# A two-direction RWKV-7 scan whose stage becomes one list of single operations

## The chip, the cores and the metric

The kernel runs on one core of a Trainium2 chip. The metric is the device time of one execution in microseconds (us), lower is better. The core's engines work side by side and each runs its own instructions in order: TensorE (PE in the profile, PEld for its weight loads), VectorE (DVE), ScalarE (ACT), GpSimd (POOL), and SyncE (SP), which here only issues DMAs. They wait for one another through semaphores. Matmul results land in PSUM, which has eight banks; the kernel hands them out through three pools: `pm` with two banks, `p2` with two, `pS` with four.

## The reference

One layer of a hybrid model on 128 context tokens and 2048 latent tokens, model width 1024:

- An RMS norm with modulation, then one input projection to eight parts of 512 channels: r, k, v, a gate, and four parts of a short gated convolution.
- Head group A (8 heads of 64 channels) is RWKV-7 time mixing, run once forwards and once backwards over the tokens. For each head a 64x64 state S is carried along: `S = S*w - (S kk)(kk*a)^T + v k^T`, and the output is `y = S r`. The two directions are summed and normalised per head; a bonus term and the gate follow.
- Both groups are joined, pass an output projection, a gated residual and a last RMS norm.

Outputs are y for all tokens and the final context states. Everything is float32.

## The kernel before, in words

Phase 1 makes the projections and writes the scan's operands to DRAM. Phase 2 is the scan. Phase 3 is the output projection; it begins inside the last three stages of the scan.

The scan runs in chunks of 64 tokens. There are 17 stages; one stage does 8 chunks for two heads in each direction, so it has two groups, 0 (forwards) and 1 (backwards). Stages go through 4 head pairs x 4 token blocks, with the context stage put in as the 16th. Inside a chunk the recurrence is turned into matrix products. For each stage:

- **M** (`partM`): per group three products from the loaded operand tile `rr` (1 MB for a group): G, F (16 matmuls each in the program) and the transpose Q; VectorE masks G and F out of PSUM, ScalarE copies Q and half of F. A small tile `dg` collects diagonal blocks of G.
- **I** (`partI`): inverts triangular 32x32 blocks. VectorE transposes `dg` into `ab` (L852); everything else is on GpSimd: the first values of `zt` (L857, L858, L860, L861), two products over 512 columns that turn `ab` (L863, L864), and 15 steps of one product (L868) and two subtractions (L871).
- **Z, c, U** (`partZ`, `partc`, `partU`): VectorE turns the inverse back into `zr`, `zd` (L916, L919); U and W are two rounds of 32 small matmuls each (L934, L941) with ScalarE copies after each, which merge blocks of 32 into 64.
- **B** (`partB`): X (L953) applies the inverse, with 8 negating ScalarE copies (L717); then eight operator tiles E of eight matmuls each (L967), each masked out of PSUM by VectorE (L968).
- **S** (`partS`): the recurrence proper. For each of 8 steps and each group, 4 matmuls E x state into `psS` (L1006), and one VectorE multiply that scales the new state into `sv` (L1019). After four steps the outputs of a group are in one bank and go to the tile `y`, by a ScalarE copy the first time a place is written, and by a VectorE addition (L1036) the second time.
- **f** (`finish`): when the four pieces of a block's `y` are there, the block is finished: square (ACT), sum per head (DVE L1070), root (ACT), reciprocal and multiply (DVE L1074, L1075), transpose on PE into `psT` (L1087), then two VectorE operations (L1090, L1092) and a store. Since the directions meet in the middle, no block is complete in the first two stages of a head pair, two are in the third and two in the fourth.

The trace counts each matmul of the program twice (an E tile is x16 there, an S step of both groups x16).

The order is written by hand: within `manual_schedule` PE, DVE and ACT run exactly in program order (the stages 0 to 13; set-up and the last three stages are placed by the framework's scheduler). The main loop goes through one stage at a time. After each of the 8 recurrence steps it takes a few pieces of the other parts, as the strings of `ORDER` say: `b` and `B` are pieces of this stage's and the next one's B, `M`, `I` belong to the stage three ahead, `Z` to the one two ahead, `W`, `U` to the next, `a` starts a waiting finish and `f` advances it by one piece. A piece is a product with its evictions, or a pair of E tiles. U, W, half of X, and all E tiles use the two banks of `p2`; M uses `pm`; S and T use `pS`.

Of the kernel before, what the change touches and what calls it, by code (L numbers as in the profile page):

```python
# [6 lines left out]
F32 = mybir.dt.float32  # L7
# [612 lines left out]
NST = 17  # L620
MORD = (("GD", 0), ("Q", 0), ("GD", 1), ("Q", 1), ("F", 0), ("F", 1))
ON_DVE = ""
LA = 3


ORDER = ("cbWUMf", "fabMWbM", "IMUflw", "fMBfyr", "Bf", "fam", "fZ", "fByNf")
LAST = ("cbUf", "bbWwf", "fWUf", "fy", "Bff", "Bfm", "ffZf", "Byf")


def phase2(K):  # L630
# [150 lines left out]
    def partL(s, gis=(0, 1)):  # L781
        if s not in sts:
            sts[s] = Ctx()
            sts[s].g = []
        st = sts[s]
        for gi in gis:
            d, units, blk = stages[s][gi]
            g = Ctx()
            st.g.append(g)
            g.d, g.units, g.blk = d, units, blk  # L790
            g.rr = B.rr()
            if blk is None:
                for k in range(4):
                    load(g.rr[:, k], d, k, units, FULL)
            else:
                p, c0 = units[0]
                src = S[f"ops{d}"][:, p * 128:(p + 1) * 128, c0 * 64:(c0 + 8) * 64]
                D(g.rr[:, 0:4].rearrange("p k u t -> p k (u t)"), src.rearrange("k p t -> p k t"))

    def partM(s, st):  # L800

        st.dg = tl([128, 16, 32], "dg", 1, O.rI)
        for gi, g in enumerate(st.g):
            g.F, g.GA, q = B.slots[s % LA][gi]
            g.Q = q[:]

        def pieces(gi, g):

            d, rr = g.d, g.rr

            def tiles(dst, w, x):

                for a in range(4):
                    for h, hr_ in enumerate((H0, H1)):
                        for e, er in enumerate((H0, H1)):
                            u = 2 * a + e
                            T.matmul(dst(h, a, er), w[hr_, u, :], x(hr_, u), start=True, stop=True)  # L817

            def banks(nm):
                return [O.pm.tile([128, 4, 128], F32, tag="m", name=f"ps{nm}{s}_{gi}_{h}") for h in range(2)]  # L820

            def transposes():
                ps = banks("Q")
                tiles(lambda h, a, er: ps[h][er, a, 0:64], rr[:, 3], lambda hr_, u: rr[hr_, 4, u, :])
                for h in range(2):
                    copy("q", g.Q[:, h * 4:h * 4 + 4], ps[h][:, :, 0:64])

            def product(dst, w, x, mask, nm, c0):
                ps = banks(nm)
                tiles(lambda h, a, er: ps[h][er, a, :].rearrange("p (a b) -> p a b", b=64), w, lambda hr_, u: x[hr_, :, u, :])  # L830
                for h in range(2):
                    if c0:
                        copy("f", dst[:, h * 4:h * 4 + 4, 0:c0], ps[h][:, :, 0:c0])
                    V.tensor_tensor(dst[:, h * 4:h * 4 + 4, c0:], ps[h][:, :, c0:], mask[:, c0:].unsqueeze(1).broadcast_to((128, 4, 128 - c0)), ALU.mult)  # L834

            def blocks():
                V.scalar_tensor_tensor(st.dg[:, gi * 8:gi * 8 + 8], g.GA[:, :, 96:128], B.hm[:, 1:2], g.GA[:, :, 64:96], ALU.mult, ALU.add)

            F = lambda: product(g.F, rr[:, 0], rr[:, 4:1:-2], B.msk[:, MF[d]], "F", 64)
            GA = lambda: product(g.GA, rr[:, 3], rr[:, 1::-1], B.mkg[:, MG[d]], "G", 0)  # L840
            return dict(Q=transposes, F=F, G=GA, D=blocks)

        ops = [pieces(gi, g) for gi, g in enumerate(st.g)]
        for piece, gi in MORD:
            for c in piece:
                ops[gi][c]()
            yield

    def partI(s, st):

        ab = tl([128, 32, 32], "ab", 2, O.rI)
        V.transpose(ab[:].rearrange("p j i -> p i j"), st.dg[:].rearrange("p u i -> p i u").unsqueeze(2).broadcast_to((128, 32, 2, 16)))  # L852
        zt = st.zt = tl([128, 16, 32], "zt", 2, O.rI)
        zf = zt[:].rearrange("p a b -> p (a b)")
        tmp = tl([128, 512], "ztmp", 1, O.rI)
        dg = tl([128, 16], "dgp", 1, O.rI)
        G.memset(zt[:], 0.0)  # L857
        G.tensor_copy(zf[:, 0:512:34], B.ph[:, 0:1].broadcast_to((128, 16)))  # L858

        G.tensor_copy(dg[:], ab[:].rearrange("p j i -> p (j i)")[:, 1:1024:66])  # L860
        G.tensor_scalar(zf[:, 1:512:34], dg[:], B.ph[:, 2:3], B.ph[:, 1:2], ALU.mult, ALU.add)  # L861
        tv = tmp[:].rearrange("p (j m) -> p j m", m=16)
        G.tensor_tensor(tv, ab[:, :, 0:32:2], dg[:].unsqueeze(1).broadcast_to((128, 32, 16)), ALU.mult)  # L863
        G.tensor_tensor(ab[:, :, 1:32:2], ab[:, :, 1:32:2], tv, ALU.subtract)  # L864
# [21 lines left out]
    def partw(s, st):  # L886

        for g in st.g:
# [5 lines left out]
            if g.blk is None or c != (2 if d == 0 else 33):  # L894
                continue
# [493 lines left out]
```

## Time and profile before

| what | us |
|---|---|
| median of three timed runs (1738.21 to 1746.28) | 1741.99 |
| the profiled execution's own time | 1734.39 |
| its span, first to last instruction | 1732.3 |
| scan, first to last state multiplication of all 17 stages (starts) | 1043.7 to 1591.3 |
| first S step of stage 0 to first S step of stage 14 (the 14 stages ordered by hand) | 407.0 |

Of the span PE is busy 91%, DVE 64%, ACT 45% and POOL 34%, but the phases differ, so these are read by stretches. The views used are: busy time by stretches (one row for each stretch: its length, then each engine's busy time and instruction count, the granted TensorE clock, the DMA share and GB/s), groups of instructions by line (busy time, mean ns of one, and the idle time before them), the timeline (start, length, engine, line, operation, with the idle time before it and what ended it), and the sums of waits. A matmul row's length in the timeline covers a run of overlapping matmuls.

### The profile page before, as it was taken

To read this page: it belongs to the slowest core of one execution; us is meant where nothing else is said; L and a number is where in the kernel's file an instruction comes from. 1 tells how busy PE (TensorE), PEld (TensorE's weight loads), DVE (VectorE), ACT (ScalarE), POOL (GpSimd) and SP (SyncE) were. 2 spreads that over 40 slices of the span, in tenths; PEclk is the share of its full clock that TensorE was granted. 3 is DMA by queue.
4 is the path that set the end of the run, shared out by engine and by line. 5 is a ranking of instruction groups with operands and counts; after the bars stand their busy time and mean duration, and the time that the engine had idled before them with its cause. 6 is when DMAs were issued, how large, how long until landed. Compare 5 with 4: busy or idle time off the path is not lost. (4 is left out here: it accounts for less than half of the span.)

```text
span 1732.3 us, 42127 instructions
## 1 busy us (share of the span) xinstructions
PE 1569.4 (91%) x17364; PEld 1437.7 (83%) x17364; DVE 1116.0 (64%) x2099; ACT 777.4 (45%) x1539; POOL 587.4 (34%) x1053
## 2 busy tenths in 40 slices
PE   6999899999888999999999989888888888889898
PEld 2898899889888999999899988777777777677686
DVE  5988897545777726458864346777767775465333
ACT  4655554323454403145521037757656565622222
POOL 0022220001222100022216427888878877122121
PEclk9999999999899999999999969989989998999899
DMA  9788887673788745367786454556545654454342
GB/s 370 220 244 231 237 243 243 222 254 94 179 193 195 193 160 184 128 166 215 199 245 225 177 123 114 155 152 181 160 146 132 166 142 125 128 171 151 134 146 91
DMA packets 204271, 313.43 MB, mean 181 GB/s; under 512 B 58024, under 2 KB 147496, under 8 KB 190000
## 3 DMA queue, kind: packets, MB, share of 16 engines
q1 hardware_dynamic: 168496, 310.61, 59.4%
q10 hardware_dynamic: 35584, 0.14, 1.3%
q8 instruction: 136, 2.23, 0.6%
q14 instruction: 55, 0.45, 0.1%
HBM read 207.79 MB, written 102.91 MB: 179 GB/s over the span
## 5 line engine op out<-in xcount | busy, mean ns | idle before, releaser
L871 POOL TENSOR_TENSOR zt<-zt,ztmp 128x30 f32<-128x30 f32 (+7 forms) x510 | 202.7, 398 | 38.8
L868 POOL TENSOR_TENSOR ztmp<-ab,zt 128x60 f32<-128x60 f32 (+7 forms) x255 | 134.3, 527 | 19.3
L1006 PE MATMUL psS<-sv,E 128*64 128x64 f32 x2176 | 101.8, 237 | 25.3 <-DVE sv L1019 12.7
L1006 PEld LDWEIGHTS psS<-sv,E 128*64 128x64 f32 x2176 | 83.8, 146 | 44.1 <-DVE sv L1019 17.5
L314 POOL TENSOR_TENSOR shk<-rawl 128x384 f32<-128x384 f32 (+1 forms) x24 | 20.4, 850 | 273.6 <-ACT rawl L310 267.7
L968 DVE TENSOR_TENSOR E<-psE,msk 128x512 f32<-128x512 f32 x136 | 89.6, 681 | 32.4 <-PE psE L967 32.3
L1325 POOL TENSOR_TENSOR z<-z,x 128x512 f32<-128x512 f32 x32 | 42.4, 1328 | 154.5 <-DVE z L1321 122.9
L1019 DVE TENSOR_TENSOR sv<-psS,pc 64x128 f32<-64x128 f32 x254 | 63.2, 278 | 47.4 <-PE psS L1006 46.8
L717 ACT ACTIVATE stf<-psX 64x512 f32<-64x512 f32 x136 | 80.3, 591 | 18.0 <-PE psX L953 15.3
L158 PE MATMUL mmv<-h,w 128*128 128x384 f32 (+1 forms) x192 | 69.5, 362 | 18.8 <-ACT rawc L317 9.9
L195 POOL TENSOR_TENSOR hsls<-sq,hshs 128x384 fp32r<-128x384 f32 (+1 forms) x24 | 32.1, 1338 | 111.6 <-ACT hshs L194 34.9
L159 PE MATMUL mmv<-h,w 128*128 128x384 f32 (+1 forms) x192 | 67.7, 353 | 0.0
L158 PE MATMUL mmg<-h,w 128*128 128x384 f32 (+1 forms) x192 | 63.4, 330 | 4.5 <-ACT ta L374 2.5
L160 PE MATMUL mmv<-h,w 128*128 128x384 f32 (+1 forms) x192 | 67.3, 351 | 0.1
L158 PE MATMUL mmc<-h,w 128*128 128x384 f32 (+1 forms) x192 | 63.9, 333 | 0.8 <-DMA w<-scr_wsp 0.8
L451 ACT ACTIVATE sg<-mmgb 128x384 f32<-128x384 f32 (+1 forms) x24 | 11.4, 474 | 118.2 <-PE mmgb L160 113.0
L158 PE MATMUL mmgb<-h,w 128*128 128x384 f32 (+1 forms) x192 | 63.0, 328 | 0.0
L159 PE MATMUL mmgb<-h,w 128*128 128x384 f32 (+1 forms) x192 | 63.0, 328 | 0.0
L159 PE MATMUL mmb<-h,w 128*128 128x384 f32 (+1 forms) x192 | 63.0, 328 | 0.0
L158 PE MATMUL mmu<-h,w 128*128 128x384 f32 (+1 forms) x192 | 62.9, 328 | 0.0
L159 PE MATMUL mmu<-h,w 128*128 128x384 f32 (+1 forms) x192 | 62.9, 328 | 0.0
L160 PE MATMUL mmc<-h,w 128*128 128x384 f32 (+1 forms) x192 | 62.9, 328 | 0.0
(313 smaller groups left out, 5217.7 us busy)
## 6 DMA issues: line engine op xcount, KB each, us to landing
w<-scr_wsp SPq DMA_DIRECT2D x68, 1024.0 KB, 6.2
scr_wsp<-w SPq DMA_DIRECT2D x34, 1024.0 KB, 5.9
rr<-scr_ops SPq DMA_DIRECT2D x32, 1024.0 KB, 7.2
scr_ops<-sp SPq DMA_DIRECT2D x160, 192.0 KB, 4.7
wr<-in_win SPq DMA_DIRECT2D x34, 512.0 KB, 7.0
x<-in_x SPq DMA_DIRECT2D x17, 512.0 KB, 3.8
wadas<-in_wada SPq DMA_DIRECT2D x8, 1024.0 KB, 15.0
stf<-scr_ops SPq DMA_DIRECT2D x32, 256.0 KB, 6.0
```

What stands on the lines that cost most here:

```text
L158: T.matmul(ps[:, :n], w[:, 0, k], hh[:, 0, k, :n], start=k == 0, stop=False)
L159: T.matmul(ps[:, :n], w[:, 0, k], hh[:, 1, k, :n], start=False, stop=False)
L160: T.matmul(ps[:, :n], w[:, 1, k], hh[:, 0, k, :n], start=False, stop=k == 7)
L195: eng.tensor_tensor(lo[:, :n], t_[:, :n], hi[:, :n].bitcast(F32), ALU.subtract)
L314: G.tensor_tensor(s[:, lo:n].rearrange("p (r c) -> p r c", c=64), rp[:, :R, 0:64], rp[:, :R, 2:66], ALU.add)
L717: P.activation(dst, src, AF.Copy, scale=-1.0)
L868: G.tensor_tensor(tv, ab[:, j:j + 2, j + 2:32].unsqueeze(1).broadcast_to((128, kn, 2, n)), zt[:, :kn, j:j + 2].unsqueeze(3).broadcast_to(( ...
L871: G.tensor_tensor(zt[:, :kn, j + 2:32], zt[:, :kn, j + 2:32], tv[:, :, r], ALU.subtract)
L968: V.tensor_tensor(g.E[n][:, k:k + 2].rearrange("p a b c -> p (a b) c"), pe[:].rearrange("p a b c -> p (a b) c"), B.msk[:, ME[g.d]].unsquee ...
L1006: T.matmul(sp[gi][r, q, hd, :], g.E[n][:, k, hd, r], sv[:, u, hd, :], start=True, stop=True)
L1019: r = V.tensor_tensor(dst, sp[gi][0:64, q], B.pc[0:64, d, 2 * p:2 * p + 2, c:c + 1].broadcast_to((64, 2, 64)), ALU.mult)
L1325: (V if last else G).tensor_tensor(z[:, cs], z[:, cs], xt[:, cs], ALU.add)
```

## The change

A stage is no longer a set of generators. Every operation has a name, and one list, `SEQ`, of 106 entries is gone through once for each **body** b. An entry `name+d` is done for stage b+d. So a body holds the S steps of its own stage (`S00` to `S70`, `S11` to `S71`; the first step of group 1, `S01+1`, stands at the end of the body before), most of X and E of the next stage, Z, c, U of the one two ahead, F and the inverse of the one three ahead, and G and Q of the one four ahead. The last figure of most names is the group; `Ev`, `Ge`, `Fe` are evictions on VectorE, `Fa`, `Qe`, `Xc`, `c`, `gh`, `bu`, `n` copies on ScalarE, `sv` the state's scaling, `y` the output of half a stage; `L`, `gsL`, `fsL`, `svL` are loads. A matmul and its eviction are thus placed apart.

A finish is cut into seven entries (`fw fr fq fm T fy fa`). `fw`, at the start of a body, takes one complete block if there is one, and the whole finish runs in that body: one at most for each body, the first in body 3.

Three more things move. The inverse's two products over 512 columns go from GpSimd to VectorE (`pre`, using `dg` as scratch), and its first values go to ScalarE (`begin`: a copy scaled by zero for the 512 columns, and two small ones that read the diagonal of `ab` directly). U and W now use banks of `pS`, and some E tiles use `pm`. U's copy goes into `zd` and no longer into a tile `bu`. There is a fifth `y` buffer. The last three stages use the same list, placed by the scheduler as before, with rules on what must come first.

```diff
-MORD = (("GD", 0), ("Q", 0), ("GD", 1), ("Q", 1), ("F", 0), ("F", 1))
...
-ORDER = ("cbWUMf", "fabMWbM", "IMUflw", "fMBfyr", "Bf", "fam", "fZ", "fByNf")
-LAST = ("cbUf", "bbWwf", "fWUf", "fy", "Bff", "Bfm", "ffZf", "Byf")
+EARLY = -9
+
+
+SEQ = """
+S00 bu+1 dg1+3 fw E101 gsL1+2 fsL1+1 S11 ab+3 Ev110 zi+3 sv11 Fm1+3 L1+4 E010 Ev101 sv00 fr fq Ev010 S21
+E100 gsL0+2 fsL0+1 W+1 sv21 S31 Fa1+3 Ev100 S10 Fe1+3 sv31 sv10 n+1 gh00+2 fm Fm0+3 L0+4 pre+3 S41 sv41 S20
+X1+1 Fa0+3 Xc01+1 sv20 I+3 Xc11+1 T S51 S30 Fe0+3 fy sv30 init+1 sv51 X0+1 y00 S40 Xc00+1 E001+1 sv40 zr+2
+S50 sv50 S61 sv61 Ev001+1 E011+1 S71 svL1+2 Xc10+1 sv71 S60 Gm0+4 sv60 y11 gh01+2 E000+1 gh11+2 zd+2 Ev011+1
+Ge0+4 c0+2 y01 S70 svL0+2 c1+2 sv70 S01+1 Ev000+1 E111+1 fa Ev111+1 Gm1+4 Qm0+4 U+2 Qe0+4 gh10+2 y10 dg0+4
+Ge1+4 sv01+1 Qm1+4 Qe1+4 E110+1
+"""
+IN_PM = "E000 E001 E011 Fm1 Gm1 Qm1 X1".split()
+IN_S = "T U W".split()
...
-        G.memset(zt[:], 0.0)
-        G.tensor_copy(zf[:, 0:512:34], B.ph[:, 0:1].broadcast_to((128, 16)))
-
-        G.tensor_copy(dg[:], ab[:].rearrange("p j i -> p (j i)")[:, 1:1024:66])
-        G.tensor_scalar(zf[:, 1:512:34], dg[:], B.ph[:, 2:3], B.ph[:, 1:2], ALU.mult, ALU.add)
-        tv = tmp[:].rearrange("p (j m) -> p j m", m=16)
-        G.tensor_tensor(tv, ab[:, :, 0:32:2], dg[:].unsqueeze(1).broadcast_to((128, 32, 16)), ALU.mult)
-        G.tensor_tensor(ab[:, :, 1:32:2], ab[:, :, 1:32:2], tv, ALU.subtract)
...
+    def begin(name, s, st, gi):
+
+        st.zt = tl([128, 16, 32], "zt", 2, O.rI)
+        zf = st.zt[:].rearrange("p a b -> p (a b)")
+        P.activation(zf.rearrange("p (a b) -> p a b", b=128), B.idt[:].unsqueeze(1).broadcast_to((128, 4, 128)), AF.Copy, scale=0.0)
+        P.copy(zf[:, 0:512:34], B.ph[:, 0:1].broadcast_to((128, 16)))
+        P.activation(zf[:, 1:512:34], pairs(st.ab), AF.Identity, bias=B.ph[:, 1:2], scale=B.ph[:, 2:3])
+
+    def pre(name, s, st, gi):
+
+        ab = st.ab
+        tv = st.dg[:].rearrange("p u i -> p (u i)").rearrange("p (j m) -> p j m", m=16)
+        V.tensor_tensor(tv, ab[:, :, 0:32:2], pairs(ab).unsqueeze(1).broadcast_to((128, 32, 16)), ALU.mult)
+        V.tensor_tensor(ab[:, :, 1:32:2], ab[:, :, 1:32:2], tv, ALU.subtract)
+
+    def inverse(name, s, st, gi):
+
+        ab, zt = st.ab, st.zt
+        tmp = tl([128, 256], "ztmp", 1, O.rI)
         for m in range(15):
             j, kn, n = 2 * m, m + 1, 30 - 2 * m
...
+    def pool_of(name, s):
+
+        if K.body == EARLY or name in IN_PM and K.body < NST - 3:
+            return O.pm, "m"
+        return (O.pS, "S") if name in IN_S else (O.p2, "s")
...
+    def ending(name, s, st, gi):
+
+        if name == "fw":
+            st.fin = pend.pop(0) if pend and K.body < NST - 3 else None
+        if st.fin is not None:
+            next(st.fin, None)
...
+        for b, n, t in order_of(range(-3, 0)):
+            K.body = b
+            do(n, t)
+        order = tc.manual_schedule(engines={mybir.EngineType.PE, mybir.EngineType.DVE, mybir.EngineType.Activation})
+        order.__enter__()
+        for b, n, t in order_of(range(0, NST - 3)):
+            K.body = b
+            do(n, t)
+        order.__exit__(None, None, None)
```

How the built programs' instructions stand, at three places. First GpSimd, at the border between two inverses (`zt` the inverse, `ab` the turned blocks, `ztmp` and `dgp` scratch). Before:

```order
L868 TENSOR_TENSOR ztmp_14829<-ab_14826,zt_14828 128x60
L871 TENSOR_TENSOR zt_14828<-zt_14828,ztmp_14829 128x15x2 x2
L860 COPY dgp_15369<-ab_15365 128x16
L861 TENSOR_SCALAR zt_15367<-dgp_15369,ph 128x16
L863 TENSOR_TENSOR ztmp_15368<-ab_15365,dgp_15369 128x512
L864 TENSOR_TENSOR ab_15365<-ab_15365,ztmp_15368 128x512
L868 TENSOR_TENSOR ztmp_15368<-ab_15365,zt_15367 128x60
```

With the change the same place on GpSimd:

```order
L909 TENSOR_TENSOR ztmp_14916<-ab_14747,zt_14751 128x112
L912 TENSOR_TENSOR zt_14751<-zt_14751,ztmp_14916 128x14x4 x2
L909 TENSOR_TENSOR ztmp_14916<-ab_14747,zt_14751 128x60
L912 TENSOR_TENSOR zt_14751<-zt_14751,ztmp_14916 128x15x2 x2
L909 TENSOR_TENSOR ztmp_15434<-ab_15265,zt_15269 128x60
```

Nothing of GpSimd's stands between the last step of one inverse and the first step of the next any more; only the 15 steps are left.

Second VectorE, around the operation that reads the transposed block `psT` of a finish. Before (stage 4):

```order
L1074 RECIPROCAL yss_12461<-yss_12461 128x8
L1075 TENSOR_TENSOR y_11375<-y_11375,yss_12461 128x512
L1019 TENSOR_TENSOR sv_12312<-psS_0_0_12524,pc 64x128
L1019 TENSOR_TENSOR sv_12318<-psS_1_0_12530,pc 64x128
L968 TENSOR_TENSOR E_12310<-psE_0_01_12540,msk 128x512
L968 TENSOR_TENSOR E_12316<-psE_1_01_12550,msk 128x512
L1090 SCALAR_TENSOR_TENSOR sg_12439<-psT_12621,gwh,sg_12439 128x512
L1019 TENSOR_TENSOR sv_12312<-psS_0_0_12524,pc 64x128
```

With the change (a body in the middle):

```order
L1131 RECIPROCAL yss_13228<-yss_13228 128x8
L1132 TENSOR_TENSOR y_10900<-y_10900,yss_13228 128x512
L899 TENSOR_TENSOR dg_13128<-ab_13189 128x512
L900 TENSOR_TENSOR ab_13189<-ab_13189,dg_13128 128x512
L1074 TENSOR_TENSOR sv_12461<-psS_1_4_13325,pc 64x128
L1074 TENSOR_TENSOR sv_12514<-psS_0_0_13162,pc 64x128
L1147 SCALAR_TENSOR_TENSOR sg_13170<-psT_1489_13406,gwh,sg_13170 128x512
L856 TENSOR_TENSOR F_10071<-psFm_8_1484_13304,msk 128x4x64
```

The two inverse products (L899, L900) now stand on VectorE between the multiply of the finish and its reading of `psT`, and the E evictions no longer do.

Third TensorE, ahead of the same transpose. Before (stage 4):

```order
L967 MATMUL psE_0_01_12540<-stg_10096,stf_10090 64x128 x8
L967 MATMUL psE_1_01_12550<-stf_10091,stg_10097 64x128 x8
L934 MATMUL psU_12566<-zr_12463,GA_10076 32x32 x16
L934 MATMUL psU_12566<-zr_12463,GA_10079 32x32 x16
L817 MATMUL psQ_0_0_12601<-rr_8831 64x64 x2
...
L1087 MATMUL psT_12621<-idt_8813,y_11375 64x2x64 x8
L1006 MATMUL psS_0_0_12524<-sv_12312,E_12310 64x64 x4
```

With the change (body 3):

```order
L1048 MATMUL psS_1_4_12285<-sv_11441,E_1371_12012 64x64 x4
L1048 MATMUL psS_0_0_12122<-sv_11496,E_1369_12001 64x64 x4
L999 MATMUL psX_4_1396_12295<-F_8828,zb 64x128 x2
...
L1144 MATMUL psT_1399_12366<-idt_8813,y_11395 64x2x64 x8
L1048 MATMUL psS_1_4_12285<-sv_11441,E_1371_12012 64x64 x4
L1048 MATMUL psS_0_0_12122<-sv_11496,E_1369_12001 64x64 x4
```

U, whose bank was one of the two that E uses, stood two places ahead of the transpose; now X, in two banks of its own, stands there, and U is near the end of the body in a bank of `pS`.

More of the change, by code (lines that the diff above doesn't have):

```diff
@@ new lines, in main @@
+                pend[:] = []
+                K.body = b
+                if b == NST - 1:
+                    for b_, n_, t_ in late:
+                        if n_[0] == "E" and b_ == b:
+                            do(n_, t_)
+                    O.l1.close()
+                    run(tail)
+                    tail = K.tail()
+                if b >= NST - 2:
+                    for f in todo:
+                        run(f)
+            do(n, t)
+            if n[0] == "S" and n[-1] == "1":
+                next(tail, None)
+                for f in todo:
+                    next(f, None)
```

570 lines of the change are left out of this document (300 added, 270 removed).

## The prediction

> **What bounds the kernel now.** I read first where the time lies (busy time by stretches), because the change touches only the scan. Columns: the stretch and its length in us, then busy us and instruction counts of PE, PEld, DVE, ACT and POOL, then the granted TensorE clock, DMA share and GB/s.
>
> ```profile
> core 0: us, PE busy (x) PEld busy (x) DVE busy (x) ACT busy (x) POOL busy (x), PEclk, DMA share, GB/s
> 1043.70:1450.70 407.00, 348.28 (x9124) 308.97 (x9123) 297.14 (x616) 264.81 (x507) 325.03 (x707) 0.94 0.54 149
> 1450.70:1594.00 143.30, 128.25 (x1467) 105.05 (x1468) 76.53 (x153) 58.39 (x109) 40.82 (x52) 0.95 0.48 144
> ```
>
> The 14 stages ordered by hand take 407.0 us, 29.1 for each, and nothing fills them: PE has work for 86% of it, at a clock of 0.94. So I cut the stretch at each turn of an inverse (the VectorE operation L916, once a stage) and counted in a second table, of `psT` alone, which finishes each piece holds (16 matmuls for one).
>
> ```profile
> 1064.00:1088.30 24.30, 23.09 (x646) 20.04 (x646) 17.57 (x39) 19.10 (x37) 21.14 (x47) 1.00 0.58 153
> 1088.30:1112.90 24.60, 22.62 (x646) 19.79 (x644) 18.98 (x40) 18.71 (x37) 21.36 (x48) 1.00 0.61 159
> 1112.90:1143.20 30.30, 24.60 (x670) 21.50 (x670) 24.64 (x54) 20.94 (x39) 26.12 (x60) 0.98 0.55 157
> 1143.20:1177.60 34.40, 29.26 (x694) 26.59 (x692) 23.73 (x48) 19.67 (x38) 27.16 (x59) 0.87 0.55 154
> 1177.60:1205.40 27.80, 24.25 (x636) 21.44 (x633) 19.12 (x42) 17.84 (x35) 21.40 (x47) 0.94 0.58 171
> 1205.40:1230.00 24.60, 22.45 (x644) 19.85 (x646) 18.61 (x41) 18.42 (x36) 21.28 (x49) 1.00 0.56 154
> ...
> 1112.90:1143.20 30.30, 1.09 (x16) 0.85 (x16) 0.75 (x1) 0.98 0.55 157
> 1143.20:1177.60 34.40, 3.07 (x32) 2.43 (x32) 1.50 (x2) 0.87 0.55 154
> ```
>
> A stage without a finish takes 24.3 to 24.6 us, with one 27.8 to 30.3, with two 34.4. PE in the plain ones is busy for 22.45 to 23.09, all but 1.2 to 2.2 us (1.8 in the mean): there TensorE is the bound, at clock 1.00. With finishes PE idles 3.6 to 5.7 us, and the clock falls. What a finish stops is seen in the sums of waits and in the timeline (start, length, and in brackets the idle time ahead).
>
> ```profile
> DVE sg L1090 <- PE psT L1087: 33.9, 10, 4.4
> PE psU L934 <- DVE E L968: 23.3, 15, 2.9
> ...
> 1151.44 1.27 DVE L968 TENSOR_TENSOR E<-psE,msk 128x512 f32<-128x512 f32 x2
> 1152.17 1.92 PE L934 MATMUL psU<-zr,GA 32*32 32x32 f32 x64 [2.52 <-DVE E L968]
> 1154.02 1.13 PE L817 MATMUL psQ<-rr 64*64 64x64 f32 x32
> 1155.08 1.97 PE L1087 MATMUL psT<-idt,y 128*64 128x128 f32 x16
> 1157.10 0.75 DVE L1090 SCALAR_TENSOR_TENSOR sg<-psT,gwh,sg 128x512 f32<-128x512 f32 x1 [4.39 <-PE psT L1087]
> ...
> 1211.63 1.20 PE L934 MATMUL psU<-zr,GA 32*32 32x32 f32 x64 [0.52 <-DVE E L968]
> 1213.39 0.68 PE L1006 MATMUL psS<-sv,E 128*64 128x64 f32 x16
> 1214.78 1.04 PE L967 MATMUL psE<-stf,stg 128*64 128x128 f32 x16
> 1218.68 0.69 PE L817 MATMUL psQ<-rr 64*64 64x64 f32 x32
> 1223.86 1.09 PE L953 MATMUL psX<-F,zb 64*64 64x128 f32 x32
> ```
>
> It is a loop of two engines. The VectorE work of the finish delays an E eviction; U shares the two banks of `p2` with E and waits 2.52 for it; Q and the transpose stand behind U, and VectorE's next instruction, L1090, waits 4.39 for that transpose, with the state's scaling `sv` behind it (the order on VectorE above). Then PE runs at a lower clock: U 1.92 where a quiet stage has 1.20, Q 1.13 against 0.69. That is the clock that the trace grants, and it costs more than the wait. So the present bound is TensorE in some stages and this hand-over in the others.
>
> **GpSimd's relief.** The groups of GpSimd in the same 407 us (busy, mean ns, idle ahead):
>
> ```profile
> L871 POOL TENSOR_TENSOR zt<-zt,ztmp 128x126 f32<-128x126 f32 (+7 forms) x417 | 163.7, 393 | 31.6
> L868 POOL TENSOR_TENSOR ztmp<-ab,zt 128x240 f32<-128x240 f32 (+7 forms) x208 | 109.6, 527 | 15.7
> L864 POOL TENSOR_TENSOR ab<-ab,ztmp 128x512 f32<-128x512 f32 x14 | 18.5, 1318 | 1.1
> L863 POOL TENSOR_TENSOR ztmp<-ab,dgp 128x512 f32<-128x512 f32 x14 | 18.2, 1298 | 0.0
> L857 POOL MEMSET zt<- 128x512 f32 x13 | 6.8, 525 | 0.0
> L861 POOL TENSOR_SCALAR zt<-dgp,ph 128x16 f32<-128x16 f32 x14 | 5.7, 406 | 1.5
> L858 POOL COPY zt<-ph 128x16 f32<-128x16 f32 x13 | 3.6, 280 | 0.1
> L860 POOL COPY dgp<-ab 128x16 f32<-128x16 f32 x14 | 2.9, 205 | 32.1 <-DVE ab L852 32.1
> ```
>
> All eight are 329.0 us busy; with the idle time between them, but without the 32.1 us of waiting for `ab`, 379, or 27.1 a stage. The last six go (55.7, with their gaps 58.4, so 4.2 a stage): 22.9 stay. By itself that is worth nothing, because the plain stages run at 24.5 with an inverse that was given out earlier, and VectorE never waits for it (the turn L916 in the next fence has 0.0 idle ahead); what it buys is that GpSimd can follow a body of 24 to 26, which at 27.1 it could not for long.
>
> **What VectorE and ScalarE take over.**
>
> ```profile
> L1092 DVE TENSOR_TENSOR sg<-sg,w 128x512 f32<-128x512 f32 x12 | 8.6, 716 | 0.5 <-DMA w<-scr_q 0.5
> L1036 DVE TENSOR_TENSOR y<-psS,y 64x512 f32<-64x512 f32 x24 | 16.6, 694 | 0.6
> L916 DVE STREAM_TRANSPOSE zr<-zt 128x512 f32<-128x512 f32 x14 | 14.9, 1068 | 0.0
> ...
> L719 ACT COPY stg<-GA 64x512 f32<-64x512 f32 x28 | 17.2, 616 | 0.5
> L1072 ACT ACTIVATE yss<-yss,geps 128x8 f32<-128x8 f32 x12 | 3.6, 301 | 8.3 <-DVE yss L1070 8.1
> ```
>
> VectorE gets two products of 128x512 with both inputs in SBUF. The nearest row is L1092, 716 ns; the other end is GpSimd's own time for them, 1298 and 1318. I take 1.4 us for the pair, since VectorE runs them as it runs L1092, and keep 2.6. Its load: the four stages from 1112.90 hold four finishes, 24.64, 23.73, 19.12 and 18.61, mean 21.5; with the pair 22.9 (24.1 at the dear end). The `y` additions, four at 0.694, come in two of four bodies, so these have 1.4 more, 24.3. ScalarE gets a fill of 512 columns (0.62 by L719) and two small operations (0.30 each by L1072): 19.1, as in the fullest plain stage, becomes 20.3, far below the rest.
>
> **What the list makes of a body.** TensorE computes the same matmuls: 22.7 (mean of 23.09, 22.62, 22.45) and 1.09 for one finish, 23.8. VectorE has 22.9, GpSimd 22.9, ScalarE 20.3. The hand-over above goes, since U is no longer in the banks of E, and the transpose stands behind X, which is in the banks of `pm`; between the finish's multiply and the reading of `psT` VectorE now has the two products and `sv`, work that doesn't wait for PE's tail. What is late next is the usual small change between PE and VectorE; I give it the 1.8 us that the plain stages show: 23.8 + 1.8 = 25.6 for a body with a finish, at a clock near 1.00. One finish at most for a body means none in bodies 0 to 2 and one in each of 3 to 13: 3 x 24.5 + 11 x 25.6 = 355.1, against 407.0: **51.9 less**. Bounds: without any wait 23.8 a body, 25 us below; with twice the wait, 20 above.
>
> The edges: the list fetches more ahead of the first body (three E tiles, G, two Q, U and an S step: 3 x 1.04 + 1.10 or so for G, taken like X, + 2 x 0.69 + 1.20 + 0.34, in all 7.1) and leaves the same kind of work out of body 13 and the last stages. I take +3, between 0 and 7. The last stages, 143.3 long with PE busy for 128.25, get one finish more and a better mixed order; I take 0, within 10 each way. Sum: -51.9 + 3 = **-48.9**. From the profiled execution's 1734.39 that gives 1685.5; it lies 7.6 under the median of the runs, so **1693**. The forecast's own range is 1672 to 1714.
>
> **Rivals.** *GpSimd becomes the bound.* VectorE's products now read SBUF twice while GpSimd works on the same inverse chain. How much that can slow GpSimd is seen in one shape, in a quiet stretch (925 to 1000) and in the scan (1130 to 1450):
>
> ```profile
> L868 POOL TENSOR_TENSOR ztmp<-ab,zt 128x252 f32<-128x252 f32 x4 | 2.5, 623 | 0.3
> ...
> L868 POOL TENSOR_TENSOR ztmp<-ab,zt 128x252 f32<-128x252 f32 x21 | 14.9, 708 | 1.6
> ```
>
> 14% more. If that came once again, 22.9 would be 26.1, over PE's 25.6, and all 14 bodies 365: 1703. Against it: the new pair adds only 1.4 us to VectorE's two-input work. The Trainium skill says (SBUF — State Buffer, section "SBUF: two separate sides") that a VectorE instruction with two SBUF inputs and a reading GpSimd instruction lock each other out for the whole instruction; by that GpSimd would lose the pair's 1.4 us, 24.3 a body, and the sum would stay; the row of 708 ns agrees in direction, not in size.
>
> *The clock stays low.* If the gaps that remain still pull the clock down, bodies look like the one at 1177.60 (27.8, clock 0.94): 11 x 27.8 + 73.5 = 379.3, so 1717. For it: that stage had just one finish. Against: 1.8 us of idle in plain stages left it at 1.00.
>
> *The finish costs what it did.* The stages from 1112.90 sum to 117.1, 19.1 over four plain ones, so 4.8 a finish. If any place of the finish does this as before, 11 x 4.8 = 52.8 come back: 343 + 52.8 = 395.8, with +3 and the finish that moves to the last stages (4.8) 1739: no change. Half a per cent, 8.7 us, is about what a measurement can tell here.
>
> *The operand load becomes the bound (slower).* Group 0's `rr` is loaded between F and G of the same body: after F0 has read the old operands, before G0 of the next stage needs the new ones.
>
> ```profile
> rr<-scr_ops SPq DMA_DIRECT2D x24, 1024.0 KB, 7.5
> ...
> wadas<-in_wada SPq DMA_DIRECT2D x8, 1024.0 KB, 15.0
> ```
>
> Between them PE has nine half S steps (0.34 each, half of 0.68), two X, two E and a transpose: 3.1 + 2.2 + 2.1 + 1.1 = 8.5, with its share of the waits 9.2. A load takes 7.5, so it is hidden by 1.7. It shows above 9.2, and the change is lost (48.9 + 8.7 over 14 bodies, 4.1) above 13.3; at 15.0, which the same size took in an earlier phase, each body is 5.8 longer and PE idle enough to lower its clock: 1693 + 81 = 1774. For it: the load stands on SP behind others, the finish's among them. Against: in the scan no 1 MB load is near 13.
>
> That the change doesn't do what it says is unlikely: the order of the built program shows the places moved.
>
> **Chances.** Forecast 0.58, GpSimd 0.12, clock 0.08: faster by over 0.5% together 0.78. The finish as before 0.11 (same). The load 0.11 (slower). The predicted time is the likeliest, 1693. The range reaches down to 1666 (no waits, and a little from the last stages) and up to 1739 (the finish as before).
>
> **What would show it.** Right: 407.0 becomes about 355; bodies are near 25.6 whether or not a block ends in them, PE's clock 0.99 or 1.00; VectorE's wait for `psT` falls from 33.9 to a few us; GpSimd has about 22.9 a body with idle time before each inverse; the two products take near 0.7 each. Wrong: L916's successor waits for GpSimd, or G for `rr` (GpSimd or load rival); the pair takes over 1.3 each; or PE's idle time stays at 4 or 5 us a body with another releaser.

## The result

The changed kernel takes 1722.96 us (median of 9 runs) beside 1738.21 of the kernel before: a ratio of **0.9895, interval 0.9869 to 0.9921**, 15 us faster. Measured a second time on another occasion the ratio was 0.9856 (0.9819 to 0.9894), 1704.3 beside 1730.9. So the gain is 1.0 to 1.4%, where 2.8% (48.9 us) was forecast. The direction was right, the size was not.

The stretches of the changed kernel's profiled execution (span 1712.9), with columns as before: the 14 bodies, from `S00` of body 0 to `S00` of stage 14, what follows up to phase 3, and some single bodies, cut again at the turns of the inverse.

```profile
1048.30:1431.90 383.60, 337.20 (x9062) 301.53 (x9059) 316.25 (x641) 274.93 (x543) 272.33 (x627) 0.97 0.60 161
1431.90:1575.00 143.10, 128.25 (x1322) 104.11 (x1318) 75.36 (x151) 54.50 (x105) 31.06 (x32) 0.89 0.45 139
...
1065.30:1089.90 24.60, 22.65 (x648) 20.49 (x646) 18.89 (x41) 18.95 (x39) 16.36 (x41) 1.00 0.54 145
1116.60:1145.20 28.60, 24.75 (x670) 21.74 (x666) 26.01 (x55) 21.18 (x42) 19.24 (x44) 1.00 0.54 150
1145.20:1171.00 25.80, 23.49 (x648) 21.00 (x650) 23.18 (x47) 16.93 (x35) 17.80 (x42) 1.00 0.55 149
1224.90:1252.70 27.80, 24.11 (x668) 21.40 (x664) 25.91 (x56) 18.83 (x38) 20.80 (x49) 1.00 0.62 161
1252.70:1283.30 30.60, 24.67 (x648) 21.93 (x648) 23.44 (x47) 19.05 (x39) 21.84 (x51) 0.96 0.64 170
1309.40:1334.00 24.60, 23.14 (x664) 21.00 (x662) 22.07 (x46) 20.72 (x42) 18.16 (x43) 1.00 0.60 171
1334.00:1364.60 30.60, 24.62 (x664) 21.55 (x660) 25.97 (x56) 20.14 (x41) 21.33 (x49) 1.00 0.76 169
1391.60:1415.70 24.10, 23.18 (x666) 21.08 (x662) 22.11 (x47) 19.35 (x39) 18.93 (x44) 1.00 0.30 86
```

The 14 bodies take 383.6 instead of 407.0, 23.4 less (forecast: 51.9). They begin 4.6 later (forecast: 3), and from stage 14 on there is nothing gained or lost (281.0 beside 281.6; forecast: 0). So nearly the whole error sits in the bodies. They no longer jump to 34 with a finish, but they are not flat at 25.6 either: 24.1 to 30.6 between turns, and the mean of all 14 is 27.4. A single profile is not exact here: in the profile of the second measurement of the same kernel body 0 begins at 1040.4 instead of 1048.3, and the 13 bodies between the turns of stages 2 and 15 take 355.6 us instead of 350.3. So the agreement of the start (4.6 for 3) says little, and differences of 5 us between the bodies of two profiles are not told from nothing.

What PE waits for in these 14 bodies, by line (busy, mean ns, idle ahead and what ended it), and the sums of two waits of other engines; the first two lines are sums of waits in the 14 stages of the kernel before:

```profile
PE psU L934 <- DVE E L968: 20.3, 14, 2.5
PE psX L953 <- issue: 9.5, 8, 2.7
...
L1048 PE MATMUL psS<-sv,E 128*64 128x64 f32 x1808 | 83.6, 229 | 10.8 <-DVE sv L1074 6.2 <-issue 4.5
L999 PE MATMUL psX<-F,zb 64*64 64x128 f32 x896 | 39.3, 293 | 19.8 <-issue 11.8 <-DVE F L856 7.9
L840 PE MATMUL psGm<-rr 64*64 64x128 f32 x832 | 33.9, 282 | 6.6 <-DVE E L1022 3.8 <-DMA rr<-scr_ops 2.7
L937 PE MATMUL psU<-zr,GA 32*32 32x32 f32 x896 | 17.7, 195 | 0.3 <-issue 0.3
L1144 PE MATMUL psT<-idt,y 128*64 128x128 f32 x176 | 12.5, 279 | 2.9 <-issue 2.9
...
DVE sg L1147 <- PE psT L1144: 11.5, 11, 3.8
POOL ztmp L909 <- DVE ab L900: 64.2, 14, 8.2
```

U's wait for an E eviction, 20.3 before (the prediction's 23.3 comes from a stretch that is 9 us longer), is gone, and VectorE's wait for `psT` fell from 33.9 to 11.5. GpSimd is idle before every inverse. What is left are 46.4 us of idle PE (383.6 less 337.2), and two causes stand out. "issue", with no releaser that the trace knows, is about 22 of them when the rows of all lines are added, over half of it at X; in the kernel before it was 16. Then comes VectorE with about 20: F, whose masking frees a bank for X, `sv` and E.

What "issue" is can be seen in the first body, on PE and on the queue of SP, and in what the DMA engines did during the wait.

```profile
1056.26 0.89 PE L999 MATMUL psX<-F,zb 64*64 64x128 f32 x24
1061.32 0.45 PE L999 MATMUL psX<-F,zb 64*64 64x128 f32 x8 [4.17 <-issue]
...
1050.94 0.54 SPq L830 DMA_DIRECT2D rr<-scr_ops  x1
1055.80 0.37 SPq L830 DMA_DIRECT2D rr<-scr_ops  x1
...
q1 hardware_dynamic: 327, 0.61, 101.9%
q8 instruction: 1, 0.02, 2.8%
...
q8 instruction: 72, 1.18, 1.4%
```

PE stops in the middle of X, after 24 of its 32 matmuls, where both banks and all operand tiles have been in use already, and the trace names no releaser. Two 1 MB loads have been issued in 4.9 us, the DMA engines are full (101.9% in the stretch from 1057.5 to 1061.3; a packet's whole time is counted where it starts, so the share can pass 100%), and in it one packet passes on the instruction queue q8. The last line is that queue over the scan, 1048 to 1432: 72 packets of 16 KB, for 18,121 recorded matmuls and weight loads of PE in the 14 bodies, about 252 for each packet. So these are PE's instructions.

That PE waits for them can be seen in the records of the single packets. In the first body the packet ends at 1059.63 and PE goes on 1.69 us later. The same holds for every stop of PE of more than 0.5 us without a releaser, between 1043 and 1440 us, in all fourteen traces of this study: each of the 135 ends 1.2 to 1.7 us after the end of a packet on q8. Such packets come about every 5 us, and of the 333 other stops of that length, which have a releaser, 12% end so. So "issue" of this size is PE waiting for its next instructions. When a packet was asked for is not recorded; that the loads hold it up is what the experiments below test.

### The profile page after: what moved, and what is told of

It is laid out like the page before. It is cut to its first block, busy times and chain, and to the rows that moved or that the text cites. A ratio compares the mean times of both kernels' runs of the same rounds, so it can differ in the third digit from the quotient of the medians.

```text
span 1712.9 us, 42020 instructions
## 1 busy us (share of the span) xinstructions
PE 1561.0 (91%) x17364; PEld 1432.1 (84%) x17364; DVE 1145.1 (67%) x2133; ACT 792.4 (46%) x1590; POOL 517.4 (30%) x951
## 5 line engine op out<-in xcount | busy, mean ns | idle before, releaser
L1048 PE MATMUL psS<-sv,E 128*64 128x64 f32 x2176 | 105.4, 233 | 16.3 <-DVE sv L1074 10.2
L1048 PEld LDWEIGHTS psS<-sv,E 128*64 128x64 f32 x2176 | 90.8, 144 | 31.4 <-issue 16.0
L1022 DVE TENSOR_TENSOR E<-psE,msk 128x512 f32<-128x512 f32 x136 | 91.5, 680 | 17.5 <-PE psE L1017 16.8
L158 PE MATMUL mmv<-h,w 128*128 128x384 f32 (+1 forms) x192 | 70.2, 366 | 19.7 <-ACT q1r L312 10.6
L999 PE MATMUL psX<-F,zb 64*64 64x128 f32 x1088 | 52.0, 302 | 19.8 <-issue 11.8
L158 PE MATMUL mmc<-h,w 128*128 128x384 f32 (+1 forms) x192 | 64.2, 335 | 0.5 <-DMA w<-scr_wsp 0.5
L159 PE MATMUL mmc<-h,w 128*128 128x384 f32 (+1 forms) x192 | 63.1, 329 | 0.0
L158 PE MATMUL mmgb<-h,w 128*128 128x384 f32 (+1 forms) x192 | 63.1, 328 | 0.0
L160 PE MATMUL mmc<-h,w 128*128 128x384 f32 (+1 forms) x192 | 63.0, 328 | 0.0
L159 PE MATMUL mmgb<-h,w 128*128 128x384 f32 (+1 forms) x192 | 62.9, 328 | 0.0
L195 POOL TENSOR_TENSOR hsls<-sq,hshs 128x384 fp32r<-128x384 f32 (+1 forms) x24 | 30.6, 1277 | 106.8 <-DMA scr_vt<-vt 41.9
L160 PE MATMUL mmgb<-h,w 128*128 128x384 f32 (+1 forms) x192 | 62.9, 327 | 0.0
```

The costliest lines, as they stand in the source:

```text
L158: T.matmul(ps[:, :n], w[:, 0, k], hh[:, 0, k, :n], start=k == 0, stop=False)
L159: T.matmul(ps[:, :n], w[:, 0, k], hh[:, 1, k, :n], start=False, stop=False)
L160: T.matmul(ps[:, :n], w[:, 1, k], hh[:, 0, k, :n], start=False, stop=k == 7)
L999: T.matmul(px[e][hr_, a, :], B.zb[er, gi * 8 + hd * 4 + a, :], g.F[er, hd * 4 + a, :], start=True, stop=True)
L1022: V.tensor_tensor(g.E[n][:, k:k + 2].rearrange("p a b c -> p (a b) c"), pe[:].rearrange("p a b c -> p (a b) c"), B.msk[:, ME[g.d]].unsquee ...
L1048: T.matmul(g.sp[i // 4][r, q, hd, :], g.E[n][:, k, hd, r], g.sv[:, u, hd, :], start=True, stop=True)
```

## The experiments

Two theories stood against each other. **V**: what PE still waits for is VectorE, which the moved products have filled. **F** (not the product F): it is the supply of instructions, which stands behind bursts of loads. And a question beside them: which part of the change brought the gain at all?

**1. The inverse's products back on GpSimd** (in the changed kernel).

```diff
-        V.tensor_tensor(tv, ab[:, :, 0:32:2], pairs(ab)...
-        V.tensor_tensor(ab[:, :, 1:32:2], ...
+        G.tensor_tensor(tv, ab[:, :, 0:32:2], pairs(ab)...
+        G.tensor_tensor(ab[:, :, 1:32:2], ...
```

> The changed kernel with the inverse's two products back on GpSimd. Theory V (what PE still waits for in a body is VectorE, which the pair has filled to 22.8 of 27.0 us): VectorE falls to 21.0 a body, PE's waits for VectorE in the scan (some 24 us) shrink by a third to a half, the 13 bodies after the first go from 27.0 to about 26.3, and the time by 8 to 12 us, unless GpSimd takes its place: it goes from 19.3 busy to 21.9, with its gaps 25.3, still below. Theory F (the waits without a releaser, 22 us, are what is lost, and VectorE has room): no change within 4 us. If the move of the pair was what the gain over the kernel before came from, the time rises by 10 or more.

Measured: 0.9899 (0.9869 to 0.9929), 1711.1 beside 1729.3. No change against the changed kernel (0.9895 and 0.9856). VectorE's busy time in the 13 bodies between the turns of stages 2 and 15 falls from 296 to 277 us, and they take 354.1, where the changed kernel's two profiles have 350.3 and 355.6. So VectorE's fill is not what holds this kernel, nor is the move what the gain came from.

**2. The masking of F ahead of the transpose.**

```diff
-X1+1 Fa0+3 Xc01+1 sv20 I+3 Xc11+1 T S51 S30 Fe0+3 fy sv30
+X1+1 Fa0+3 Xc01+1 sv20 Fe0+3 I+3 Xc11+1 T S51 S30 fy sv30
```

> The changed kernel with one entry of the list moved: the masking of F of group 0 (Fe0) ahead of the finish's transpose and its reading, so that X of group 0 finds its bank free. In the changed kernel X waits 0.72 us for that masking in 11 bodies, 7.9 us. Theory V: this wait ends, nothing else comes in its place, and the time falls by 6 to 9 us. Rival: the body has another bound right behind it (VectorE's row, the state's scaling), and the time falls by less than 3 us, with PE's waits for sv up by what this one lost.

Measured: 0.9855 (0.9813 to 0.9896), 1702.7. The changed kernel itself gave 0.9856 in its second measurement, so alone this is not told from no change. In its trace X has lost the wait for F, and waits longer without a releaser:

```profile
L999 PE MATMUL psX<-F,zb 64*64 64x128 f32 x896 | 36.9, 293 | 18.2 <-issue 18.1
```

**3. A quarter of each operand load.** 

```diff
+        few = 0 <= K.body and s < NST - 2
...
-            p, c0 = units[0]
+            p, c0 = (sts[3].g[gi].units if few else units)[0]
+            k1 = 1 if few else 4
...
-            D(g.rr[:, 0:4]...., src.rearrange("k p t -> p k t"))
+            D(g.rr[:, 0:k1]...., src.rearrange("k p t -> p k t")[:, 0:k1])
```

The operands of these stages are read from stage 3's place, and three quarters of them are left out, so the outputs are not those of the layer; only the time is of use.

> The changed kernel with three quarters of each 1 MB operand load of stages 4 to 14 left out (and all operands of these stages taken from stage 3's place, so that the values stay finite): 256 KB instead of 1024 KB for each group. All instructions of the engines stay. Theory F (the instruction fetches of PE stand behind these loads in the DMA engines): the waits without a releaser fall from 22 us to under 8, the wait for rr (2.7) goes, and the time falls by 15 to 20 us. Theory V: these waits stay near 22 us, and the time falls by less than 5 us.

Measured: 0.9738 (0.9704 to 0.9772), 1678.6: some 26 to 33 us below the changed kernel (0.9856 to 0.9895 of the same 1729.3), more than theory F expected. Its 13 bodies between the turns of stages 2 and 15, and X:

```profile
1053.60:1383.50 329.90, 304.27 (x8508) 273.24 (x8504) 296.97 (x601) 255.42 (x508) 263.21 (x586) 0.99 0.42 119
...
L1003 PE MATMUL psX<-F,zb 64*64 64x128 f32 x896 | 34.7, 277 | 7.9 <-DVE F L860 7.9
```

In these 13 bodies the waits without a releaser fall from 18 us (18.1 and 18.2 in the changed kernel's two profiles) to 4.5, those for VectorE stay (20, from 17), the clock is 0.99, and a body takes 25.4 (329.9 over 13). Of the 20.4 us that these bodies lose against the changed kernel's first profile 12.9 are idle time of PE and 7.5 its busy time, at a clock of 0.99 instead of 0.98. The instructions of the engines are the same. So the loads cost the changed kernel this much, though PE waits only 2.7 us in all for their data.

**4. The kernel before, U and W in other banks.**

```diff
-        pu = O.p2.tile([128, 16, 32], F32, tag="s", ...
+        pu = O.pS.tile([128, 16, 32], F32, tag="S", ...
-        pw = O.p2.tile([128, 16, 32], F32, tag="s", ...
+        pw = O.pS.tile([128, 16, 32], F32, tag="S", ...
```

> The kernel before with U and W in banks of the pool of the state's products, and nothing else changed. My account of the kernel before (U waits for the bank of an E tile, and a loop of PE and VectorE forms around the finish): U's wait of 20.3 us for E goes, half of VectorE's 33.9 us for psT with it, the clock rises from 0.94 to 0.96, and the time falls by 15 to 25 us, about as much as the whole change brought. Rival: what keeps VectorE back is the transpose standing behind Q and U in program order, whatever the bank: U then waits for sv or a bank of psS, and the time falls by less than 6 us.

Measured: 0.9902 (0.9867 to 0.9937), 1709.3. **Two lines bring as much as the whole change.** VectorE's wait for `psT` falls as it does there, U waits for nothing, and the clock rises from 0.94 to 0.98:

```profile
DVE sg L1090 <- PE psT L1087: 11.2, 7, 3.6
...
L934 PE MATMUL psU<-zr,GA 32*32 32x32 f32 x960 | 18.3, 193 | 0.0
...
1056.30:1408.50 352.20, 313.64 (x8514) 277.42 (x8516) 278.75 (x578) 246.88 (x473) 305.69 (x666) 0.98 0.59 163
...
1063.95:1445.40 381.45, 326.81 (x8518) 289.94 (x8520) 277.97 (x578) 247.22 (x474) 306.29 (x668) 0.94 0.55 151
1065.30:1415.60 350.30, 311.75 (x8510) 278.98 (x8506) 296.06 (x600) 254.38 (x506) 250.15 (x578) 0.98 0.58 157
1053.77:1409.33 355.56, 314.80 (x8506) 281.04 (x8504) 296.02 (x600) 255.64 (x508) 254.49 (x583) 0.97 0.58 156
```

Its 13 stages take 352.2; the same stretch (last three lines) takes 381.5 in the kernel before and 350.3 and 355.6 in the changed one's two profiles.

**5. The changed kernel again**, as a control for the next three.

> The changed kernel itself, beside the next three on one chip, so that differences of a few us between them can be read. Expected as measured: 0.9895 of the kernel before, within 0.003.

Measured: 0.9856 (0.9819 to 0.9894), 1704.3 beside 1730.9; a little faster than the 0.003 either way that was expected.

**6. The operand load cut in two.**

```diff
-... Gm1+4 Qm0+4 U+2 Qe0+4 ... Ge1+4 sv01+1 Qm1+4 Qe1+4 ...
+... Gm1+4 Qm0+4 K0+5 U+2 Qe0+4 ... Ge1+4 sv01+1 Qm1+4 K1+5 Qe1+4 ...
...
-            D(g.rr[:, 0:4]...
+            D(g.rr[:, k0:k0 + 3:2]...
```

`K` loads planes 1 and 3 (k0 = 1), `L` keeps planes 0 and 2 (k0 = 0).

> The changed kernel with each 1 MB operand load cut in two: the planes that only G and Q read (1 and 3) are loaded as soon as Q has read them, at the end of the body before, and the other two stay where they were. The same bytes, two more loads a body, but half of the burst (2 MB in some 8 us) moved into the stretch in which the DMA engines stand idle. Theory F (instruction fetches stand behind the burst): the waits without a releaser fall from 22 us to 10 to 15 and the time by 6 to 14 us. Theory B (it is the number of bytes over the whole body that counts, not their bunching): no change within 4 us.

Measured: 0.9788 (0.9754 to 0.9821), 1690.6: 13.7 below the control. The 13 bodies take 335.3, where the control has 355.6. The bytes are the same, so their bunching is what costs.

```profile
1056.41:1391.67 335.26, 306.84 (x8510) 274.24 (x8506) 294.87 (x601) 254.40 (x506) 255.88 (x582) 0.99 0.61 164
...
L1001 PE MATMUL psX<-F,zb 64*64 64x128 f32 x832 | 33.4, 278 | 10.9 <-DVE F L858 7.2 <-issue 3.6
...
rr<-scr_ops SPq DMA_DIRECT2D x44, 512.0 KB, 5.5
```

In the 13 bodies "issue" falls from 18 to 9 us, at X in the control from 8.2 to 3.6; the wait for F, which stood behind it, is what is left at X.

**7. The cut and the masking together.**

> The two edits together: the loads cut in two, and the masking of F of group 0 ahead of the finish's transpose. If the two waits are separate, the gains add: 12 to 20 us under the changed kernel. If one only uncovers the other, as the single profile of the masking alone suggests (its X waited as long without a releaser as it had for VectorE), the sum stays at the larger one, 6 to 14.

Measured: **0.9721 (0.9693 to 0.975), 1682.9**: 21.4 below the control, 7.8 below the cut alone. Where these 7.8 come from is not shown. The wait for F (7.2 in run 6) is gone from X, but most of it comes up again: the wait for `sv` goes from 2.3 to 7.2 and "issue" from 9.0 to 10.6, and the 13 bodies are only 2.7 shorter (332.6 for 335.3). The two profiles differ by 10.6 in all; the rest of it lies before and after these bodies:

```profile
1052.97:1385.53 332.56, 305.35 (x8508) 273.53 (x8504) 296.05 (x601) 255.58 (x508) 257.75 (x581) 0.99 0.62 165
...
L1001 PE MATMUL psX<-F,zb 64*64 64x128 f32 x832 | 31.3, 280 | 3.4 <-issue 3.3
L1050 PE MATMUL psS<-sv,E 128*64 128x64 f32 x1664 | 74.7, 226 | 9.8 <-DVE sv L1076 7.2 <-issue 2.5
```

This is the fastest version that leaves nothing out, 48 us below the kernel before.

**8. The same with the inverse's products on GpSimd.**

> The same two edits and the inverse's two products back on GpSimd. If VectorE has become the bound of the bodies with four y additions (26 us busy there), taking 1.8 us from it now shows: 5 to 10 us less than without it. If GpSimd at some 25 us a body is the bound then, it is slower by up to 5. If neither, the same within 3 us, as it was in the changed kernel.

Measured: 0.9825 (0.9802 to 0.9848), 1700.4: 17.5 slower, more than any expectation. But not in the bodies, which take 333.4 as against 332.6. Two waits at the border to the last stages, the second behind the first, make most of it up:

```profile
DVE zr L922 <- POOL zt L914: 17.7, 1, 17.7
...
PE psE L1019 <- DVE E L1024: 16.5, 1, 16.5
```

The last inverse ends late on GpSimd, and there, where the framework's scheduler places the instructions, its turn on VectorE stands ahead of an E eviction that PE needs. In run 7 VectorE waits 4.9 at the same place, and PE 0.5 behind it. So in the bodies the move to VectorE is worth nothing, and what it saved here is one wait after them. How much of that is the inverse and how much the place that the scheduler chose was not taken apart.

**9. The kernel before with the banks and the cut.** (Q of a group is followed by the load of planes 1 and 3 of its next stage.)

```diff
+            if piece == "Q" and s + 1 < NST:
+                partL(s + 1, (gi,), True)
```

> The kernel before, with U and W in the banks of the state's products and each operand load cut in two (planes 1 and 3 as soon as Q of that group is through). No list, GpSimd with all of its work. If the list and the moved products of the inverse bring nothing of their own, this does for the kernel before what the cut did for the changed one: 8 to 14 us below the banks alone, a ratio to the kernel before of about 0.982. Rival: GpSimd, 27.1 us a stage, is the bound once the banks are free (the 13 stages of the banks alone took 352, 27.1 each): then the cut brings less than 4 us, 0.989.

Measured: 0.9876 (0.9831 to 0.9921), 1708.1. The cut brings nothing to be measured here. But GpSimd is not shown to be the reason, as I gave it for this case: no turn of the inverse waits for it, though it is nearly full itself (in these 13 stages it waits only 3.8 us for `ab`). "Issue" does fall, from 19.9 to 12.9, less than in run 6; the wait that grows is that of the state steps, for `sv` from 12.1 to 17.4. And the cut does not do the same here: Q of group 1 stands near F in the old order, so three of the four half loads are issued within 4 us (first lines, on the queue of SP), where run 6 takes 9 for three.

```profile
1090.39 0.37 SPq L803 DMA_DIRECT2D rr<-scr_ops  x1
1097.41 3.95 SPq L803 DMA_DIRECT2D rr<-scr_ops  x3
...
L1013 PE MATMUL psS<-sv,E 128*64 128x64 f32 x1666 | 74.7, 233 | 21.2 <-DVE sv L1026 17.6 <-issue 2.1 <-DVE E L975 1.0
```

**10. The same with the inverse's first part moved as in the change.**

> The same with the inverse's two products on VectorE and its first values on ScalarE, as the change has them. If GpSimd was the bound in the run above, stages go from 27 to some 26 and the time falls by 10 to 15 us; if not, the same within 4 us. What the changed kernel with both edits has beyond this one is the list's own part.

Measured: 0.9967 (0.994 to 0.9994), 1720.8: 12.7 slower than without. The pair stands right behind the turn into `ab` there, VectorE is late for F, and PE waits for it:

```profile
L822 PE MATMUL psF<-rr 64*64 64x128 f32 x832 | 40.4, 309 | 20.7 <-DVE F L839 20.7
```

So the list by itself brings nothing over the banks (run 4), but it bears more: with the cut of the loads it reaches 0.9788 (run 6), where the old order stays at 0.988, and it takes the pair on VectorE at no loss (run 1), where the old order loses 13 us. How much of the first is the order, and how much the better spacing of the half loads that the list allows, was not taken apart.

**11. The changed kernel with U and W in the old banks.**

```diff
-IN_S = "T U W".split()
+IN_S = "T".split()
```

> The changed kernel with U and W back in the two banks that E uses. If those banks are what the change's gain came from, the gain goes: a ratio of 0.996 to 1.004, PE's wait of U for an E eviction is back with 10 to 20 us. If the list has taken the loop apart by itself (U stands near the end of a body, far from the transpose), at most 4 us are lost, 0.987 to 0.990.

Measured: 0.9995 (0.9959 to 1.003), 1728.4. The whole gain goes; the 13 bodies take 378.9. The wait is not the one that I named, though: in the new order U's bank is held by Q's copy, not by an E eviction, and U and W in turn hold the banks of E and F until ScalarE has copied them (`zd`, `zb`). These waits for ScalarE sum to 22 us; the changed kernel's profile has none of them.

```profile
L937 PE MATMUL psU<-zr,GA 32*32 32x32 f32 x832 | 15.6, 192 | 9.4 <-ACT Q L869 9.4
L1017 PE MATMUL psE<-stf,sth 128*64 128x128 f32 x444 | 29.8, 275 | 6.0 <-ACT zd L940 5.3 <-DVE GA L856 0.7
L840 PE MATMUL psFm<-rr 64*64 64x128 f32 x832 | 34.2, 277 | 4.0 <-ACT zb L948 4.0
```

**12. The best version without the additions of y.**

```diff
-            V.tensor_tensor(y[r], src, y[r], ALU.add)
+            P.copy(y[r], src) if 0 <= K.body < NST - 3 else V.tensor_tensor(...)
```

This leaves out the sum of the two directions in the bodies 0 to 13, so the outputs are not those of the layer.

> The best kernel so far (both edits) with each VectorE addition of y in the bodies 0 to 13 replaced by a ScalarE copy of the same shape, so the sum of the two directions is left out. Theory: VectorE bounds the bodies that hold four additions (26 us busy of 27 to 29), and the others are at PE's floor. Then the former fall from 27.8 to 24.8 and the time by 15 to 20 us. Rival: these bodies are long for another reason that comes with them (loads, ScalarE), and less than 5 us go.

Measured: 0.9684 (0.9637 to 0.9731), 1675.0, beside 0.9721 with the additions: 6 us, a third of what I expected, and the intervals overlap. The 13 bodies go from 332.6 to 326.0; the three with four additions from 27.8, 27.1 and 29.1 to 26.6, 25.5 and 27.7, not to 24.8. PE's waits for VectorE fall, and "issue" grows from 10.6 to 15.5. So VectorE is part of what is left in the bodies with additions, but not their bound alone.

## Why the prediction was right and wrong

**Direction and range** held: faster, and 1723 lies between 1666 and 1739, a range that reached from no waits at all to no gain. The size did not: 15 us (27 in the second measurement) for 48.9.

**What the finish cost.** That U in the banks of E ties PE and VectorE into a loop was right, and more right than the prediction made of it: moving U and W alone, in the old order, brings 0.9902, and taking that one move out of the change leaves 0.9995. I had credited the list with it as much as the banks. VectorE's wait for `psT` fell to 11.5, not to "a few us"; with a quarter of the operand loads (run 3) it is 3.5.

**The step that failed** is "I give it the 1.8 us that the plain stages show". I took the idle time of PE in the three fastest stages before and carried it to every body as a constant. It measured 3.3 (46.4 over 14). The 14 bodies are 28.5 us longer than forecast (383.6 for 355.1): 21.2 of these are idle time of PE (46.4 for 14 x 1.8 = 25.2), and 7.3 its busy time (337.2 for 329.9), at a granted clock of 0.97 where I had taken 1.00; in the 11 pieces between turns that hold a finish PE is busy for 24.1, where 23.8 was forecast. VectorE and GpSimd came out near the forecast: in these 11 VectorE was busy for 23.4 (22.9 forecast), GpSimd for 19.5 with some 3.4 of gaps (22.9 forecast). What I didn't ask is what the 1.8 was made of. I called it "the usual small change between PE and VectorE"; in the three plain stages 0.85 of it in the mean was "issue" already. The list issues the loads about as bunched as the old order did: two 1 MB loads and four of 256 KB in some 7 us, while the DMA engines stand idle elsewhere in the body. In the 13 bodies the wait was 15.7 before, 18.1 with the change, and 19.9 in run 4, which keeps the old order: it came up as the hand-over went. When the burst was taken away (run 3), the 13 bodies took 329.9; the forecast for the same bodies, 2 x 24.5 + 11 x 25.6, is 330.6. That this is so near is in part luck: the idle time of PE there is 25.6 us, 2.0 a body, most of it VectorE's.

**What is late next** was not looked for. That the X ahead of the transpose stands in `pm` is right, but it is X of group 1. X of group 0 shares `p2` with F of group 0, and the masking of that F stands on VectorE behind the reading of `psT`: 0.72 in each of 11 bodies. The list shows this place. What it costs stays open: moved alone (run 2) there is no gain to be seen, and with the loads spread the time falls by 7.8 us, but the bodies by 2.7 (run 7 against 6).

**The clock rival** came true in small. The granted clock of the 14 bodies is 0.97, three of the 13 pieces between turns have 0.94, and PE's busy time is 7.3 above the forecast, where the rival had 24 more in all.

**The load rival** had the right resource and the wrong mechanism. I asked whether a load lands before its reader; it mostly does (9.4 us at the median in the changed kernel, just above the 9.2 at which I let it show, and PE waited only 2.7 us in all for `rr`). PE waited 22 us for instructions while data loads filled the DMA engines: spreading the loads (run 6) halves this wait, and a quarter of their bytes (run 3) leaves a quarter of it.

```profile
rr<-scr_ops SPq DMA_DIRECT2D x24, 1024.0 KB, 9.4
```

**GpSimd's relief** I costed at nothing by itself, with the words that it lets GpSimd follow a shorter body. In the bodies neither shows: the pair can go back (run 1), even at 25.6 a body (run 8: 333.4 for 13 bodies). The rival that GpSimd becomes the bound is refuted by the 64.2 us that it waits for `ab`, and its steps kept their lengths: 394 and 529 ns in the mean, 393 and 527 before.

**The pair on VectorE** cost more than I took, 1.82 instead of 1.4, within the bounds: the second product ran as the row that I had chosen, the first, with its strided and repeated operands, did not.

```profile
L899 DVE TENSOR_TENSOR dg<-ab 128x512 f32<-128x512 f32 x14 | 15.8, 1128 | 0.0
L900 DVE TENSOR_TENSOR ab<-ab,dg 128x512 f32<-128x512 f32 x14 | 9.7, 694 | 0.5
```

With it the bodies with four additions have 26.0 of VectorE, not 24.3, and they are long (28.6, 27.8, 30.6). But they are not long for this alone: the one from 1252.70, with 23.4 of VectorE, takes 30.6 too, with 2.9 of "issue" and 2.0 of waiting for `rr`. Run 12 prices the additions at some 6 us in the best version.

## What to carry to other kernels

Before an idle time of the bounding engine is carried over as a constant, ask for each piece of it what ended it, and what "issue" in the middle of a run of like instructions can be: here it was PE waiting for its instructions, and it followed the bunching of the loads. When a change has several parts, undo each of them alone: here two lines on banks were the gain, and the new order only showed its worth once the loads were spread. A wait of 0.7 us that is measured in each body is not 0.7 us of gain while another stands behind it. And compare the stretch that an edit touches, not only the total: in run 7 the two profiles differ by 10.6 us, the 13 bodies by 2.7.

## What was not expected of the hardware

PE stopped for up to 4.2 us inside a run of matmuls, with no operand or bank that the trace names as missing, while the DMA engines were full (101.9%). The sum of such waits was 18 us in 13 bodies, 9 with the same bytes spread, and 4.5 with a quarter of the operand bytes. All 135 of them that are longer than 0.5 us, in fourteen traces, end 1.2 to 1.7 us after a 16 KB packet on the instruction queue. The Trainium skill, "Runtime: NRT & Kernel Launch", section "Instruction fetch mechanics", says that an engine's instructions come in blocks of 16 KiB over a DMA queue of its own, and that the cost of crossing a block is mostly hidden. The blocks and the queue agree with this trace (72 packets of 16 KB, 1.18 MB, in the scan); that the cost is hidden does not, when transfers fill the DMA engines. That the instructions come late because they stand behind the loads fits runs 3 and 6, which changed the loads; no run here changed the fetch alone, and how long a packet waits for its turn is not in the traces.
